# VectorE's small instructions with one SBUF tensor and pointer scalars, the head norm's constant folded into its factor, its row product and one-column moves on GpSimd

## The chip, the cores and the metric

The kernel runs on one core of a Trainium2 chip. The time is the device time of one execution in microseconds (us); lower is better. The engines are named as the profile names them: PE is TensorE (PEld its weight loads), DVE is VectorE, ACT is ScalarE, POOL is GpSimd, SP is SyncE, whose queue issues all DMAs here.

## The reference, cut to what matters

Two post-norm layers work on 1024 positions of 1024 features. A layer projects h to q, k, v and u. Eight heads of differential attention use q, k, v; each head has two softmax maps p0 and p1 over 1024 keys. u goes through a two-dimensional Fourier transform and a small linear map. Both halves are multiplied with w_o, and two layer norms stand around a SwiGLU feed-forward. The change concerns these lines of the attention:

```
p = softmax(q k^T * scale - slope * dist)          # for c = 0, 1
a = p[0] - lam * p[1]
o = a v                                            # 64 columns per head
o = o * rsqrt(mean(o^2, over the 64 columns) + 1e-5)
o = o * subln_g * (1 - lam_init)
```

and the mean, variance and shift of each layer norm. All of it is float32.

## The kernel before, in words

Positions are cut in 8 tiles of 128 partitions. Each float32 factor of a matmul is split into a high and a low part in the type fp32r that the matmuls read (`split`, L126 and L129: ScalarE writes the high part, VectorE or GpSimd subtracts), and three matmuls (`mm3`, L132 to L134) make one product.

`attention` runs over 64 blocks, 8 heads of 8 query tiles. For a block and both maps, TensorE makes the scores (L306), VectorE adds the distance and takes the row minimum (`bias_min`, L314), ScalarE takes the exponential with its row sum in a column of z (`expo`, L324). `combine` then brings both maps together without dividing: L329 takes the reciprocal of the second sum, L330 makes the column rho = z0 * (-lambda) / z1, L333 the column z0 squared on GpSimd, and E0 + rho * E1 is made in one of two ways. By the table `OFF`, 94 of the 128 blocks of both layers use two GpSimd instructions (L335, L336), the other 34 one VectorE instruction (L338). The sum is transposed on TensorE (L344), split (L351 on ScalarE, L356 on VectorE) and multiplied with v (L366).

Since nothing was divided by z0, the head norm takes it in: `norm_a` squares the head's output `onat` on GpSimd (L395), sums its 64 columns (L397), divides by 64 (L398), adds 1e-5 z0^2 (L399), takes the power -1/2 on GpSimd (L401) and multiplies the rows of `onat` with it (L402). It is called once for each of the first six heads of a layer (8 columns of factors, 512 of values) and twice for each of the last two (4 and 256). The column `subg`, the product of subln_g and 1 - lam_init, comes in later, when the heads are transposed (L416, L431).

Between the blocks stand pieces of other work from a generator, `step`, four at each block: projections of the next heads, and in the last quarter of a layer the `fourier` part. It sums and mirrors u on GpSimd (L549, L552), transposes and splits, and for each of four groups makes a pair of tiles fh and fl by a first transform, takes out of both the column at 384 (L606 copies it twice side by side into `mid`, L607 writes zero in its place), and multiplies them on TensorE in a second step. The first product reads their first half, the second their second half with the zero.

`layer_norm` (L170 to L185) makes mean and variance on VectorE (L173, L175), adds 1e-5 (L177), takes the power on GpSimd (L178) and makes the shift -mean * factor (L179); ScalarE, VectorE and GpSimd then apply it (L181 to L183).

The order on each engine is not written by hand: a scheduler places the instructions by its own model of times, within the limits that `step` gives. So a change of a few instructions may move others. Each engine runs its instructions in order.

Of the kernel before, what the change touches and what calls it, by code (L numbers as in the profile page):

```python
# [16 lines left out]
ALU = mybir.AluOpType  # L17
# [47 lines left out]
def encoder(ctx: ExitStack, tc: tile.TileContext, x, ln_in_g, ln_in_b, w_in, lam_params, subln_g,  # L65
# [35 lines left out]
    def load(o, i):  # L101
        nc.sync.dma_start(out=o, in_=i)

# [1 line left out]
    ident = sb.tile([P, P], F32, tag="ident", name="ident")  # L105
    make_identity(nc, ident)
    zero = sb.tile([P, 2], F32, tag="zero", name="zero")
# [28 lines left out]
    def load_params():  # L136
        lamp = blk("raw", (P, DEPTH, 4 * HD))
        lamm = blk("raw", (P, DEPTH, 2, HD))
        for l in range(DEPTH):
            load(bfT[:, l, :], b_f[l].rearrange("(g p) -> p g", p=P))  # L140
            for half in range(2):
                load(subg[half * VD:(half + 1) * VD, l:l + 1], subln_g[l].rearrange("(d o) -> d o", o=1))
            load(lamp[:, l, :], lam_params[l].rearrange("a d -> (a d)").partition_broadcast(P))
        lv = lamp.rearrange("p l (a b d) -> p l a b d", a=2, b=2)
        for l in range(DEPTH):
            nc.vector.tensor_tensor(out=lamm[:, l], in0=lv[:, l, :, 0, :], in1=lv[:, l, :, 1, :], op=ALU.mult)
            nc.vector.tensor_reduce(out=lams[:, l, :], in_=lamm[:, l], op=ALU.add, axis=AX.X)
            nc.scalar.activation(lams[:, l, :], lams[:, l, :], AF.Exp)
            nc.vector.tensor_tensor(out=nlam[:, l:l + 1], in0=lams[:, l, 1:2], in1=lams[:, l, 0:1], op=ALU.subtract)
            nc.vector.tensor_scalar_add(nlam[:, l:l + 1], nlam[:, l:l + 1], -LAM_INIT[l])  # L150
            nc.vector.tensor_scalar_mul(subg[:, l:l + 1], subg[:, l:l + 1], 1.0 - LAM_INIT[l])

    def load_dist(act=False):
        dist = blk("dist", (P, 2048), F16)
# [15 lines left out]
    def layer_norm(r, gb, eng=None, store=None):  # L170
        st = small([P, 2, 6], "bst", 4)
        for k in range(2):
            nc.vector.bn_stats(out=st[:, k, :], in_=r[:, k * 512:(k + 1) * 512])  # L173
        mv = small([P, 4], "bmv", 4)
        nc.vector.bn_aggr(out=mv[:, 0:2], in_=st)  # L175
        rs, nmr = mv[:, 2:3], mv[:, 3:4]
        nc.vector.tensor_scalar_add(rs, mv[:, 1:2], EPS)  # L177
        nc.gpsimd.tensor_tensor(out=rs, in0=rs, in1=mhalf, op=ALU.pow)  # L178
        nc.vector.scalar_tensor_tensor(out=nmr, in0=mv[:, 0:1], scalar=-1.0, in1=rs, op0=ALU.mult, op1=ALU.mult)  # L179
        for c in [slice(0, D)] if store is None else [slice(0, D // 2), slice(D // 2, D)]:  # L180
            nc.scalar.activation(r[:, c], r[:, c], AF.Identity, bias=nmr, scale=rs)  # L181
            nc.vector.tensor_tensor(out=r[:, c], in0=r[:, c], in1=gb[0][:, c], op=ALU.mult)
            (eng or nc.gpsimd).tensor_tensor(out=r[:, c], in0=r[:, c], in1=gb[1][:, c], op=ALU.add)  # L183
            if store is not None:
                load(store[:, c], r[:, c])  # L185
# [140 lines left out]
    def combine(blk_):  # L326
        z, es, n = blk_["z"], blk_["e"], blk_["n"]
        rho = small([P, 1], "rho", 6)
        nc.vector.reciprocal(rho, z[:, 1:2])  # L329
        nc.vector.scalar_tensor_tensor(out=rho, in0=z[:, 0:1], scalar=nlam[:, blk_["l"]:blk_["l"] + 1], in1=rho,  # L330
                                       op0=ALU.mult, op1=ALU.mult)
        z2 = blk_["head"]["z2"][:, blk_["qt"]:blk_["qt"] + 1]
        nc.gpsimd.tensor_tensor(out=z2, in0=z[:, 0:1], in1=z[:, 0:1], op=ALU.mult)  # L333
        if n % OFF[n // 16][0] < OFF[n // 16][1]:
# [57 lines left out]
    def norm_a(hd, q0, n):  # L392
        onat = hd["onat"][:, q0:q0 + n, :]
        sq = blk("on", (P, n, VD))
        nc.gpsimd.tensor_tensor(out=sq, in0=onat, in1=onat, op=ALU.mult)  # L395
        rs = small([P, n], "rs", 2)
        nc.vector.tensor_reduce(out=rs, in_=sq, op=ALU.add, axis=AX.X)  # L397
        nc.vector.tensor_scalar_mul(rs, rs, 1.0 / VD)  # L398
        nc.vector.scalar_tensor_tensor(out=rs, in0=hd["z2"][:, q0:q0 + n], scalar=EPS, in1=rs, op0=ALU.mult,  # L399
                                       op1=ALU.add)  # L400
        nc.gpsimd.tensor_tensor(out=rs, in0=rs, in1=mhalf.broadcast_to([P, n]), op=ALU.pow)  # L401
        nc.vector.tensor_tensor(out=onat, in0=onat, in1=rs.unsqueeze(2).broadcast_to([P, n, VD]), op=ALU.mult)  # L402

    def emit_half(l, h, hd, half):
        rows = slice((h % 2) * VD, (h % 2) * VD + VD)
# [122 lines left out]
    def fourier(l):  # L528
# [26 lines left out]
        for g in range(NG):  # L555
# [47 lines left out]
                  fl[:, :, 256:512].rearrange("p a (b c) -> p a b c", b=2), o, nc.scalar, nc.vector)  # L603
            mid = small([P, 2, 2], "mid", 4, F32R)
            for part, t in enumerate((fh, fl)):
                nc.vector.tensor_copy(out=mid[:, part, :], in_=f32(t[:, 1, 384:385]).broadcast_to([P, 2]))  # L606
                nc.vector.tensor_copy(out=t[:, 1, 384:385], in_=zero[:, 0:1])  # L607
            A = [t[:, 2, g * P:(g + 1) * P] for t in (hTh, hTl)]
            nB = [t[:, 2, 512 + g * P:512 + (g + 1) * P] for t in (hTh, hTl)]
            Bp = [t[:, 3, g * P:(g + 1) * P] for t in (hTh, hTl)]  # L610
# [114 lines left out]
            4: [("g0", 1), ("u0", 1)], 5: [("g0", -1), ("g1", 1)], 6: [("u1", 1)], 7: [("g0", 1)]}  # L725

    class Up:
        """gate | up projection of all positions as a 2 x 2 block product in seven block products:
        block rows are gate and up columns, the contraction and the positions are cut in halves."""

        def __init__(self, l, hs):
            self.l, self.hs = l, hs
# [116 lines left out]
    CHAIN = [("2", "11"), ("1", "11"), ("6", "12"), ("7", "22"), ("4", "21"), ("5", "22"), ("3", "12")]  # L849

    def down7(l, hs, up, pairs):
        """down projection of pairs of feature tiles, each a 2 x 2 block product in seven block products
        (block rows are the halves of the positions, block columns those of the output)."""
        B = up.B

        def fetch(n, name):
# [254 lines left out]
```

## Time and profile before

| | |
|---|---|
| median of 3 runs | 2510.63 us (2510.26 to 2516.24) |
| span of the profiled execution | 2509.6 us |
| PE busy | 2383.1 us, 95% |
| DVE busy | 1943.9 us, 77% |
| POOL busy | 1807.4 us, 72% |
| ACT busy | 1227.2 us, 49% |
| chain that ended last | PE 76%, DVE 11%, ACT 5%, POOL 3% |

The span reaches from the first to the last instruction of the program. The page gives no other time for the profiled execution, so the span stands for it; it lies 1.0 us under the median. A layer's attention runs from about 85 to 530 us and from 1323 to 1760 us, its output projection and first norm follow for some 90 us, and the feed-forward takes the rest. Busy shares are means over these stages, so they are read by stretch below. Some one-column instructions last microseconds in this profile: time that an engine spends inside an instruction counts as busy, whatever it waits for there, and shows as a long duration and not as idle time.

### The profile page before, as it was taken

Reading aid. Unit: us, or ns where it says so; the run is one execution under the profiler, and the core shown is the slowest. Engines: PE = TensorE matmul, PEld = TensorE weight load, DVE = VectorE, ACT = ScalarE, POOL = GpSimd, SP = SyncE. Lnnn points to the kernel's source line nnn. Section 1 sums busy time; section 2 is a strip of 40 time slices with the busy share of each in tenths; the row PEclk is TensorE's granted clock in tenths of the full one; section 3 lists DMA queues with packets and bytes.
Section 4 is the critical chain, followed back from the end, with each engine's and each line's share of the span. In section 5 each row is a group of like instructions: output and inputs, shape, how many; then the busy total and the mean of one; then the engine's idle time right before and its main releaser. Section 6 shows DMA issues by size and latency. Waiting matters only on the chain.

```text
span 2509.6 us, 33322 instructions
## 1 busy us (share of the span) xinstructions
PE 2383.1 (95%) x11636; PEld 1951.8 (78%) x11636; DVE 1943.9 (77%) x3003; ACT 1227.2 (49%) x2252; POOL 1807.4 (72%) x1459
## 2 busy tenths in 40 slices
PE   6999998799999999999999999888999999999997
PEld 5888776677888888888788877667778888888886
DVE  7688888756578887888768898886566887878878
ACT  4577676633344343343437766666253343333442
POOL 5476667655798888888535766676578888888873
PEclk8999999899999999999999999999999999999999
DMA  6431340231112111111324232305021111211112
GB/s 219 93 97 47 89 114 27 84 122 30 51 51 61 54 55 55 51 55 56 98 85 103 72 83 73 103 26 174 25 63 39 55 56 58 59 51 55 51 34 97
DMA packets 185783, 180.04 MB, mean 72 GB/s; under 512 B 25872, under 2 KB 149264, under 8 KB 185616
## 3 DMA queue, kind: packets, MB, share of 16 engines
q1 hardware_dynamic: 185616, 177.92, 24.7%
q8 instruction: 92, 1.51, 0.3%
q14 instruction: 75, 0.61, 0.1%
HBM read 124.39 MB, written 19.92 MB: 58 GB/s over the span
## 4 chain that ended last, share of the span: by engine, by line
PE 76%; DVE 11%; ACT 5%; issue 3%; POOL 3%; DMA 2%; SPq 0%; DVEq 0%; POOLq 0%; ACTq 0%
PE mm L134 9%; PE mm L132 9%; PE mm L133 9%; PE S L132 7%; PE S L133 7%; PE S L134 7%; PE tr L134 6%; PE tr L132 6%; PE tr L133 6%; PE mm L366 3%; DVE E L314 3%; PE S L306 3%; PE tr L344 2%; ACT E L324 2%; DVE aT L356 1%
## 5 line engine op out<-in xcount | busy, mean ns | idle before, releaser
L931 DVE TENSOR_TENSOR v<-S,v 128x512 f32<-128x512 f32 x504 | 333.6, 684 | 59.6 <-PE S L134 59.2
L324 ACT ACTIVATE E<-E,mn 128x1024 f32<-128x1024 f32 x256 | 295.5, 1155 | 103.6 <-DVE mn L314 101.8
L314 DVE CUSTOM_DVE_ANT_0 E<-S,dist 128x1024 f32<-128x1024 f32 x256 | 309.4, 1216 | 31.7 <-PE tr L344 12.1
L336 POOL TENSOR_TENSOR E<-E,E 128x1024 f32<-128x1024 f32 x94 | 225.6, 2400 | 2.8
L129 POOL TENSOR_TENSOR stk<-raw,stk 128x512 fp32r<-128x512 f32 x138 | 197.8, 1434 | 23.7 <-ACT stk L126 23.5
L132 PE MATMUL S<-w,st 128*128 128x512 f32 x544 | 212.8, 391 | 0.2
L133 PE MATMUL S<-w,st 128*128 128x512 f32 x544 | 212.9, 391 | 0.0
L134 PE MATMUL S<-w,st 128*128 128x512 f32 x544 | 212.1, 391 | 0.0
L818 DVE TENSOR_TENSOR su<-su,tr 128x512 f32<-128x512 f32 x176 | 116.4, 681 | 120.0 <-PE tr L134 116.5
L132 PE MATMUL mm<-hTh,w 128*128 128x512 f32 (+1 forms) x480 | 194.6, 405 | 13.6 <-DVE w L129 5.9
L129 POOL TENSOR_TENSOR st<-stq,st 128x512 fp32r<-128x512 f32 x126 | 194.7, 1546 | 14.7 <-ACT st L126 11.8
L356 DVE TENSOR_TENSOR aT<-tr,aT 128x512 fp32r<-128x512 f32 x256 | 172.5, 683 | 37.6 <-ACT aT L351 36.9
L134 PE MATMUL mm<-hTh,w 128*128 128x512 f32 (+1 forms) x480 | 185.0, 385 | 0.8 <-POOL w L129 0.6
L306 PE MATMUL S<-stq,stk 128*128 128x512 f32 x512 | 170.0, 422 | 15.4 <-DVE mn L314 15.1
L133 PE MATMUL mm<-hTl,w 128*128 128x512 f32 (+1 forms) x480 | 183.4, 382 | 0.2 <-DVE hTl L129 0.2
L351 ACT CAST aT<-tr 128x512 fp32r<-128x512 f32 x256 | 147.0, 585 | 66.7 <-PE tr L344 47.7
L129 POOL TENSOR_TENSOR stk<-dist,stk 128x512 fp32r<-128x512 f32 x88 | 116.2, 1320 | 77.5 <-ACT stk L126 77.4
L126 ACT CAST stk<-raw 128x512 fp32r<-128x512 f32 x138 | 85.4, 619 | 176.1 <-PE tr L134 116.8
L344 PE MATMUL tr<-ident,E 128*128 128x128 f32 x1024 | 158.1, 280 | 9.3 <-DVE aT L356 5.7
L335 POOL TENSOR_SCALAR E<-E,rho 128x1024 f32<-128x1024 f32 x94 | 105.7, 1124 | 82.3 <-DVE rho L330 47.6
L129 POOL TENSOR_TENSOR stk<-on,stk 128x512 fp32r<-128x512 f32 x88 | 123.2, 1400 | 53.8 <-ACT stk L126 53.8
L126 ACT CAST stk<-dist 128x512 fp32r<-128x512 f32 x90 | 56.0, 622 | 209.1 <-PE tr L134 126.4
(343 smaller groups left out, 7146.2 us busy)
## 6 DMA issues: line engine op xcount, KB each, us to landing
on<-in_w_gu SPq DMA_DIRECT2D x88, 256.0 KB, 2.9
raw<-in_w_gu SPq DMA_DIRECT2D x88, 256.0 KB, 2.9
raw<-in_w_in SPq DMA_DIRECT2D x64, 256.0 KB, 3.3
stq<-in_w_down SPq DMA_DIRECT2D x36, 256.0 KB, 2.8
stk<-st SPq DMA_DIRECT2D x64, 128.0 KB, 2.3
stk<-su SPq DMA_DIRECT2D x64, 128.0 KB, 2.4
stq<-st SPq DMA_DIRECT2D x64, 128.0 KB, 2.4
stq<-su SPq DMA_DIRECT2D x64, 128.0 KB, 2.5
```

The lines of the kernel that those rows point to most:

```text
L129: lo_eng.tensor_tensor(out=lo, in0=src, in1=f32(hi), op=ALU.subtract)
L132: nc.tensor.matmul(o, ah, bh, start=start, stop=False, skip_group_check=more)
L133: nc.tensor.matmul(o, ah, bl, start=False, stop=False, skip_group_check=more)
L134: return nc.tensor.matmul(o, al, bh, start=False, stop=stop, skip_group_check=more)
L306: anchor[0] = nc.tensor.matmul(s[:, half * 512:half * 512 + 512], qs[:, qt * P:qt * P + P], ks[:, half * 512:half * 512 + 512], start=True ...
L314: nc.vector.tensor_tensor_reduce(out=e, in0=s, in1=blk_["dist"][:, 896 - P * qt:896 - P * qt + S], op0=ALU.add, op1=ALU.min, scale=2.0 ** ...
L324: nc.scalar.activation(e, e, AF.Exp, bias=blk_["mn"][c], scale=-1.0, accum_out=blk_["z"][:, c:c + 1])
L336: nc.gpsimd.tensor_tensor(out=es[0], in0=es[0], in1=es[1], op=ALU.add)
L344: anchor[0] = nc.tensor.transpose(pt[:, j, :], blk_["e"][0][:, c0:c0 + P], ident)
L351: nc.scalar.copy(grp["aT"][kh][0][:, :, qq * P:qq * P + P], blk_["pt"][kh])
L356: nc.vector.tensor_tensor(out=lo[:, :, qs], in0=blk_["pt"][kh], in1=f32(hi[:, :, qs]), op=ALU.subtract)
L931: nc.vector.tensor_tensor(out=dst, in0=o, in1=dst, op=ALU.add)
```

## The change

L330 and L179 had two SBUF tensors and a scalar (`scalar_tensor_tensor`). Both become `tensor_scalar`: one tensor and two scalars, which are columns in SBUF read through a pointer (in L179 one of them a constant). L398 goes: with 64 times the sum of squares in its place, the constant in L399 is multiplied by 64, and the missing factor sqrt(64) = 8 is taken into `subg` at the start. L402, L606 and L607 are given to GpSimd. Comments and two docstrings go too. From L399 on, the lines of the changed kernel are one lower: its L398 to L401 are L399 to L402 of before, its L605 and L606 are L606 and L607, its L548 is L549.

```diff
-            nc.vector.tensor_scalar_mul(subg[:, l:l + 1], subg[:, l:l + 1], 1.0 - LAM_INIT[l])
+            nc.vector.tensor_scalar_mul(subg[:, l:l + 1], subg[:, l:l + 1], math.sqrt(VD) * (1.0 - LAM_INIT[l]))
...
-        nc.vector.scalar_tensor_tensor(out=nmr, in0=mv[:, 0:1], scalar=-1.0, in1=rs, op0=ALU.mult, op1=ALU.mult)
+        nc.vector.tensor_scalar(out=nmr, in0=mv[:, 0:1], scalar1=rs, scalar2=-1.0, op0=ALU.mult, op1=ALU.mult)
...
-        nc.vector.scalar_tensor_tensor(out=rho, in0=z[:, 0:1], scalar=nlam[:, blk_["l"]:blk_["l"] + 1], in1=rho,
-                                       op0=ALU.mult, op1=ALU.mult)
+        nc.vector.tensor_scalar(out=rho, in0=rho, scalar1=z[:, 0:1], scalar2=nlam[:, blk_["l"]:blk_["l"] + 1],
+                                op0=ALU.mult, op1=ALU.mult)
...
-        nc.vector.tensor_scalar_mul(rs, rs, 1.0 / VD)
-        nc.vector.scalar_tensor_tensor(out=rs, in0=hd["z2"][:, q0:q0 + n], scalar=EPS, in1=rs, op0=ALU.mult,
+        nc.vector.scalar_tensor_tensor(out=rs, in0=hd["z2"][:, q0:q0 + n], scalar=EPS * VD, in1=rs, op0=ALU.mult,
                                        op1=ALU.add)
         nc.gpsimd.tensor_tensor(out=rs, in0=rs, in1=mhalf.broadcast_to([P, n]), op=ALU.pow)
-        nc.vector.tensor_tensor(out=onat, in0=onat, in1=rs.unsqueeze(2).broadcast_to([P, n, VD]), op=ALU.mult)
+        nc.gpsimd.tensor_tensor(out=onat, in0=onat, in1=rs.unsqueeze(2).broadcast_to([P, n, VD]), op=ALU.mult)
...
-                nc.vector.tensor_copy(out=mid[:, part, :], in_=f32(t[:, 1, 384:385]).broadcast_to([P, 2]))
-                nc.vector.tensor_copy(out=t[:, 1, 384:385], in_=zero[:, 0:1])
+                nc.gpsimd.tensor_copy(out=mid[:, part, :], in_=f32(t[:, 1, 384:385]).broadcast_to([P, 2]))
+                nc.gpsimd.tensor_copy(out=t[:, 1, 384:385], in_=zero[:, 0:1])
```

The feed-forward keeps its order on every engine. In the attention stages the scheduler places things anew. Two places:

VectorE in the first layer, at the third Fourier group (434 to 446 us of the profile). The number behind a name tells one tile of that name from another; a tile of before has in the changed kernel a number some 6 lower, so E_4801 is E_4795 there. Before:

```order
L314 ISA mn_4832 128x1
L402 TENSOR_TENSOR on_3986<-on_3986,rs_4509 128x512
L329 RECIPROCAL rho_4937<-z_4825 128x1
L330 SCALAR_TENSOR_TENSOR rho_4937<-z_4825,nlam,rho_4937 128x1
L338 SCALAR_TENSOR_TENSOR E_4801<-E_4833,rho_4937,E_4801 128x1024
L129 TENSOR_TENSOR st_4576<-mm_4602,su_4575 128x2x256
L606 CAST mid_4663<-su_4575 128x2
```

The same blocks in the changed kernel:

```order
L329 RECIPROCAL rho_4930<-z_4819 128x1
L330 TENSOR_SCALAR rho_4930<-rho_4930,z_4819,nlam 128x1
L129 TENSOR_TENSOR w_4527<-mm_4547,w_4526 128x512
L338 SCALAR_TENSOR_TENSOR E_4795<-E_4827,rho_4930,E_4795 128x1024
L129 TENSOR_TENSOR st_4570<-mm_4571,su_4569 128x2x256
L390 TENSOR_TENSOR on_4688<-mm_4578,on_4688 128x128
```

L402 and L606 have left VectorE; L338 has moved ahead of the first L129 that writes st_4570, which stood ahead of L402 before.

GpSimd a little later, at the fourth group (464 to 472 us of the profile before). Before, L606 and L607 of this group stand on VectorE, and GpSimd has:

```order
L333 TENSOR_TENSOR z_1015_4701<-z_5100 128x1
L401 TENSOR_TENSOR rs_4873<-rs_4873,mhalf 128x4
L335 TENSOR_SCALAR E_5108<-E_5108,rho_5171 128x1024
L333 TENSOR_TENSOR z_1015_4701<-z_5148 128x1
L336 TENSOR_TENSOR E_5093<-E_5093,E_5108 128x1024
L129 TENSOR_TENSOR hTl<-raw_4905,hTh 128x256
```

In the changed kernel:

```order
L400 TENSOR_TENSOR rs_4867<-rs_4867,mhalf 128x4
L401 TENSOR_TENSOR on_4688<-on_4688,rs_4867 128x256
L605 CAST mid_4874<-st_4776 128x2
L335 TENSOR_SCALAR E_5101<-E_5101,rho_5164 128x1024
L336 TENSOR_TENSOR E_5086<-E_5086,E_5101 128x1024
L606 CAST st_4776<-zero 128x1
L605 CAST mid_4874<-su_4777 128x2
L333 TENSOR_TENSOR z_1015_4695<-z_5141 128x1
L606 CAST su_4777<-zero 128x1
L129 TENSOR_TENSOR hTl<-raw_4898,hTh 128x256
```

The row product and the four one-column instructions have come in; both zeros stand behind L335 and L336, and the second also behind L333, which waits for an exponential of ScalarE.

## Rows read from the trace of the kernel before

**Rows 1.** Windows: busy us (and instructions) of each engine, granted clock, DMA.
```profile
core 0: us, PE busy (x) PEld busy (x) DVE busy (x) ACT busy (x) POOL busy (x), PEclk, DMA share, GB/s
85.00:260.00 175.00, 172.26 (x977) 144.12 (x976) 153.15 (x294) 128.98 (x252) 117.67 (x101) 1.00 0.33 78
260.00:380.00 120.00, 111.61 (x620) 89.89 (x619) 103.41 (x186) 83.43 (x156) 77.80 (x65) 1.00 0.38 100
380.00:530.00 150.00, 122.33 (x677) 99.15 (x678) 113.78 (x202) 89.45 (x186) 96.78 (x125) 0.90 0.30 95
...
620.00:1230.00 610.00, 608.94 (x2655) 495.40 (x2654) 469.47 (x597) 245.93 (x430) 510.91 (x366) 1.00 0.19 55
...
1620.00:1760.00 140.00, 118.41 (x672) 94.44 (x672) 106.30 (x197) 89.74 (x185) 95.83 (x124) 0.93 0.31 100
```
**Rows 2.** Single lines: count, min/median/max ns, first and last start, shapes.
```profile
L330 DVE SCALAR_TENSOR_TENSOR rho<-z,nlam,rho x128: 201/220/5349, 93.2 to 1725.8; 128x1 f32<-128x1 f32 x128
...
L329 DVE RECIPROCAL rho<-z x128: 146/158/166, 92.0 to 1724.6; 128x1 f32<-128x1 f32 x128
...
L618 DVE SCALAR_TENSOR_TENSOR hTl<-mm,bfT,hTh x8: 203/205/215, 478.2 to 1716.0; 128x1 fp32r<-128x1 f32 x8
...
L177 DVE TENSOR_SCALAR bmv<-bmv x40: 93/150/156, 6.5 to 2501.2; 128x1 f32<-128x1 f32 x40
...
L179 DVE SCALAR_TENSOR_TENSOR bmv<-bmv x40: 143/159/2250, 7.4 to 2502.7; 128x1 f32<-128x1 f32 x40
```
**Rows 3.** Groups by line and shape: count | busy us, mean ns | idle us before.
```profile
L330 DVE SCALAR_TENSOR_TENSOR rho<-z,nlam,rho 128x1 f32<-128x1 f32 x128 | 63.6, 497 | 2.5
...
L338 DVE SCALAR_TENSOR_TENSOR E<-E,rho,E 128x1024 f32<-128x1024 f32 x34 | 59.2, 1741 | 0.7
...
L402 DVE TENSOR_TENSOR on<-on,rs 128x512 f32<-128x512 f32 x12 | 29.4, 2449 | 0.0
...
L398 DVE TENSOR_SCALAR rs<-rs 128x8 f32<-128x8 f32 x12 | 13.3, 1105 | 0.1
...
L395 POOL TENSOR_TENSOR on<-on 128x512 f32<-128x512 f32 x12 | 12.5, 1042 | 15.9 <-DVE on L390 14.7 <-DVE rho L329 1.1
...
L606 DVE CAST mid<-su 128x2 fp32r<-128x2 f32 x4 | 2.1, 531 | 0.0
```
**Rows 4.** Timeline of VectorE, 430 to 462: start us, us, line, operation.
```profile
434.80 3.81 DVE L402 TENSOR_TENSOR on<-on,rs 128x512 f32<-128x512 f32 x1
...
438.97 1.28 DVE L338 SCALAR_TENSOR_TENSOR E<-E,rho,E 128x1024 f32<-128x1024 f32 x1
...
445.53 0.14 DVE L607 CAST st<-zero 128x1 fp32r<-128x1 f32 x1
...
454.28 5.35 DVE L330 SCALAR_TENSOR_TENSOR rho<-z,nlam,rho 128x1 f32<-128x1 f32 x1
459.66 1.28 DVE L338 SCALAR_TENSOR_TENSOR E<-E,rho,E 128x1024 f32<-128x1024 f32 x1
```
**Rows 5.** Timeline of GpSimd in the same stretch.
```profile
434.98 2.39 POOL L336 TENSOR_TENSOR E<-E,E 128x1024 f32<-128x1024 f32 x1
...
453.23 0.22 POOL L333 TENSOR_TENSOR z<-z 128x1 f32<-128x1 f32 x1
453.38 3.37 POOL L129 TENSOR_TENSOR hTl<-raw,hTh 128x256 fp32r<-128x256 f32 x6
...
457.25 2.36 POOL L336 TENSOR_TENSOR E<-E,E 128x1024 f32<-128x1024 f32 x1
```
**Rows 6.** Timeline of TensorE: in brackets its idle us before, and what ended it.
```profile
447.50 0.48 PE L133 MATMUL mm<-st,hTh 128*128 128x512 f32 x1
...
461.60 3.78 PE L366 MATMUL mm<-aT,v 128*128 128x256 f32 x16 [6.63 <-DVE w L129]
```
**Rows 7.** The chain that ended last: start us, us, engine and line.
```profile
600.74 1.25 DVE bmv L179
...
2493.19 2.17 DVE bmv L179
```

## The prediction

> **What bounds the kernel now.** I read the busy time by stretch first [rows 1]. In the feed-forward stretch from 620 to 1230 us (its twin runs from 1850 to 2460) TensorE is busy 608.9 of 610 us at the full granted clock, and the change touches nothing there. What can be won lies in the two attention stages, 85 to 530 and 1323 to 1760. In the first of them TensorE stands idle 175 - 172.3 = 2.7 us, then 120 - 111.6 = 8.4 us, then 150 - 122.3 = 27.7 us [rows 1]: it gets worse as the projections that fill its time run out and the Fourier part, which VectorE and GpSimd prepare, takes their place. [...]
>
> The second view is the spread of single lines [rows 2]. L330 writes one column; half of its 128 runs take 0.22 us or less, the longest 5.35. L329, the reciprocal just ahead of it, reads one SBUF tensor and never takes over 0.166. L330 reads two SBUF tensors, z and rho. The third view, the timelines, shows what it waits for: it starts at 454.28 while GpSimd runs six L129 in a row, after which come a short L395 (left out there) and L336 without a pause [rows 5]; it ends at 459.63, when L336 (457.25 + 2.36) ends [rows 4]. Behind it stand L338 and the L129 that TensorE needs, and TensorE is idle 6.63 us before 461.60 [rows 6]. So a VectorE instruction with two SBUF tensors waits until GpSimd has run dry, and everything behind it on VectorE waits too.
>
> **The change, part by part.** *L330* keeps its count and gets a form with one tensor, rho, and two pointer scalars. The waits in it are 128 x (0.497 - 0.220) = 35 us [rows 2, 3]. The trace has no one-tensor instruction with two pointers. The nearest: L618 reads one SBUF tensor and one pointer beside PSUM, and its eight runs take 203 to 215 ns; L177 is the same instruction kind with constants, 93 to 156 ns, never longer [rows 2]. So the new one should cost 0.15 to 0.22, I take 0.2; the upper bound is that it still waits, and nothing is gained. Of the 35 us a part is only handed on: in 34 of the 128 blocks L338 (two SBUF tensors of 1024 columns, unchanged) comes behind L330 [rows 3]. At 454.28 it stands directly behind [rows 4], and without L330's wait it would itself wait until GpSimd's L336 ends at 459.61: 5.1 of the 35 us stay. Following the long ones through in the same way I leave 15 us handed on and 20 us gone.
>
> *L179* gets the same form. Its median is 0.159, its longest run 2.25 [rows 2]; seven of 40 wait. Four of these lie on the chain of waits that ended last: 1.25 us at 600.74, two like it (in the second layer's norm after attention, and in the first norm of all), and 2.17 at 2493.19 [rows 7]. The one at 2493 stands in the tail, where the next instructions need no second SBUF tensor, so its 2.0 us are won; the other three give 1.1 each if VectorE's next work is ready. Between 0 and 5.3 us; I take 4.
>
> *L398 goes, and L399 takes the constant.* L398's twelve runs on 8 columns took 1.105 us on average [rows 3], nearly all waiting. L399 behind it has two SBUF tensors (z2 and rs) and inherits that wait, so 20 x 0.165 = 3 us of plain work are saved, no more.
>
> *L402 moves to GpSimd.* VectorE loses 12 x 2.449 = 29.4 us [rows 3] and about 4 us for the eight of half size, 33 us, of which some two thirds is waiting: at 434.80 it took 3.81 [rows 4] while GpSimd ran L336 from 434.98 [rows 5]. Here too L338 follows (438.97), and would wait for the same L336 and what is behind it; I count 8 us as handed on, 25 gone. GpSimd gains the instruction. Its price there isn't shown; the square of the same tile, L395, takes 1.04, and half of L336 is 1.2 [rows 3, 5]. I take 1.2, so 12 x 1.2 + 8 x 0.6 = 19 us over both layers. In 380 to 530 GpSimd is busy 96.8 of 150 us [rows 1], so most of this is covered; what is queued behind it are L335 and L336, whose result TensorE transposes. I charge 2 us in all. Nobody waits for L402's own result except the store and, for the last two heads, the transposes after the attention.
>
> *L606 and L607 move to GpSimd.* The first cost up to 0.53 us on average in their group of four [rows 3]; with the zeros (0.14, [rows 4]) 9 us leave VectorE. On GpSimd a one-column move costs about 0.2, like L333 there [rows 5]: 32 x 0.2 = 6 us. The wait that this adds is the third rival below.
>
> So VectorE gets rid of 20 + 25 + 3 + 7 = 55 us in two attention stages. How much reaches the end goes by TensorE's idle time in each stretch. 85 to 260: at most 2.7 us, and mostly behind other lines; 0.7 per layer. 260 to 380: 1.3 per layer, since what L398 waited L399 will wait. The last stretches: VectorE is busy 113.8 of 150 us, and TensorE's idle spells there end with VectorE's copies. About 10 us of VectorE time per layer really go there; half of it, 5 us per layer, should reach TensorE, the rest meets the next wait. **Sum:** -4 (L179) - 1.4 - 2.6 - 10 + 2 (GpSimd) = -16 us. The sum is a difference to the profiled execution, whose span is 2509.6; the median of the runs is 2510.6, 1.0 above. **Forecast: 2495 us.** The scheduler also stirs the order in the attention stages; I give that no sign, and it is in the range.
>
> [...] In the trace L398, a one-tensor instruction with a constant, waits as the two-tensor ones do when it has 8 columns (1.105 us), while L177 with one column never does [rows 2, 3]. [...]
>
> **The rivals.** *First, the wait is handed on almost whole.* L338, L399 and L182 keep two SBUF tensors, and GpSimd has 25 us more work to wait for. For it: at both long waits in [rows 4] an L338 stands within three instructions. Against it: 94 of 128 blocks have no L338. Then 4 us of L179 and some 2 us remain: 2505. *Second, the new form still waits*, as L398 does with one tensor: L402 and the moves are about half of the 55 us, so half of the attention's 14 us is left, less the 2 on GpSimd: 5 us, 2506. L177 and L618 speak against it.
>
> *Third, slower: the zero columns come late from GpSimd.* At 445.53 VectorE writes the zero, and TensorE reads that tile at 447.50 [rows 4, 6]: 1.8 us of cover. In the new order the zeros of a layer's fourth group stand on GpSimd behind L335 and L336, of which L336 alone is 2.4 us [rows 5], and one of them behind L333, which waits for an exponential. It decides where more than 1.8 us stand ahead. If it happens in all eight groups at 2.4 us each, 19 us, and the clock drops with TensorE's idle time as it did in 380 to 530, 5 us more, against 8 us that still go: about 2526. In most groups the copies are the first that GpSimd takes after its sums, so I give it little.
>
> [...]
>
> **How the numbers follow.** Forecast (2486 to 2503) 0.43; more comes back (below 2486) 0.20; handed on 0.20; the form still waits 0.04; slower 0.13. A measurement of this kernel tells about 0.3%, 7.5 us, from no change. Faster by more than that is the first two, 0.63; within it handed on and the form, 0.24; slower 0.13. The range reaches from 2474, where half of the idle time of the last stretches and most of the clock's loss were won, to 2514, which takes in both cases of no change; I leave 0.08 below and 0.12 above. The largest unknown is how much L338 inherits, between 15 us and 35 us of L330's waits.
>
> **What would show it.** L330's longest run at 0.25 us or less, and L179's: the form is free. L338's mean above its 1.74 us of now [rows 3] by what L330 lost: handed on. The last attention stretches shorter by about 5 us each, and 85 to 260 hardly at all: the sum is right by stretch. GpSimd's zero copies as what ended TensorE's idle time: the third rival. The forecast is wrong if L330 still has runs above 1 us, or if L338 and L399 together gain more than 30 us.

## The result, and the profile after

| | before | changed |
|---|---|---|
| median of the runs, one chip | 2510.45 us | 2485.53 us (2483.11 to 2488.56) |
| ratio, 95% interval | | 0.9895 [0.9875, 0.9916] |
| span of the profiled execution | 2509.6 us | 2486.8 us |
| mean granted clock over the span | 0.982 | 0.988 |
| VectorE / GpSimd / TensorE busy, us | 1943.9 / 1807.4 / 2383.1 | 1862.5 / 1839.9 / 2366.5 |

The kernel is faster by 1.05%, 25 us between the medians. A second comparison (experiment 5) gave 0.9874 [0.9858, 0.9891], 31 us, and a profile with a span of 2478.6 us at a clock of 0.990. The two intervals overlap; both profiles are used below, and the one of experiment 5 is called the second profile.

The first view is the one by stretches, of the changed kernel; the columns are those of [rows 1].

```profile
85.00:260.00 175.00, 168.89 (x938) 140.19 (x937) 141.95 (x285) 126.52 (x246) 117.85 (x99) 0.99 0.31 74
260.00:380.00 120.00, 112.75 (x635) 93.78 (x636) 91.58 (x183) 83.34 (x159) 88.13 (x76) 0.97 0.41 106
380.00:530.00 150.00, 128.30 (x742) 103.15 (x741) 106.90 (x193) 95.22 (x193) 106.22 (x144) 0.98 0.30 97
620.00:1230.00 610.00, 607.25 (x2637) 493.81 (x2636) 472.45 (x593) 245.40 (x427) 510.79 (x366) 1.00 0.19 57
1620.00:1760.00 140.00, 117.69 (x662) 95.42 (x662) 92.04 (x164) 81.78 (x164) 101.56 (x128) 0.96 0.32 100
```

Beside [rows 1]: in 380 to 530 us TensorE's idle time went from 27.7 to 21.7 us and the granted clock from 0.90 to 0.98. In 1620 to 1760 us the idle time stayed (21.6 and 22.3 us), and the clock went from 0.93 to 0.96. It isn't all gain: in 85 to 260 TensorE is idle 6.1 us instead of 2.7, and in 260 to 380 the clock fell from 1.00 to 0.97.

Fixed stretches of the two profiles don't hold the same work (380 to 530 has 677 matmuls of TensorE before and 742 after). So here are the same pieces of work in each kernel, cut at the first score matmul (L306) of a block, up to the last L366 of a layer, in us:

| stage | before | L330 alone (experiment 1) | changed, first and second profile |
|---|---|---|---|
| start, to the first block | 86.5 | 86.6 | 84.0, 82.6 |
| layer 1, blocks 1 to 24 | 126.6 | 127.0 | 132.8, 130.5 |
| layer 1, blocks 25 to 48 | 147.2 | 143.4 | 143.3, 142.8 |
| layer 1, blocks 49 to 64 | 158.5 | 157.3 | 145.3, 143.2 |
| from there to layer 2's first block | 805.3 | 801.7 | 803.3, 802.9 |
| layer 2, blocks 1 to 24 | 127.3 | 126.9 | 127.4, 127.1 |
| layer 2, blocks 25 to 48 | 147.2 | 144.4 | 144.0, 145.4 |
| layer 2, blocks 49 to 64 | 150.9 | 148.1 | 146.4, 144.8 |
| from there to the end | 760.1 | 761.5 | 760.3, 759.3 |

Most of the gain lies in the last 16 blocks of layer 1. What the clock takes can be bounded from the span and its mean: the share below 1.00, times the span. Before that is 2509.6 x 0.018 = 45 us, in the changed kernel 2486.8 x 0.012 = 30 us, in its second profile 2478.6 x 0.010 = 25 us. These are upper bounds, since they count time at the lower level (0.50; the traces of the kernel before and of the changed one have this level and 1.00 alone) in which TensorE is idle or, behind its last matmul, done (5.7, 4.4 and 5.0 us of them). In the trace before, 128x512 matmuls back to back start 0.43 us apart at 0.50 (441.93 to 443.21) and 0.23 apart at 1.00 (700.12 to 702.91), so about half of the busy time at the lower level is lost: 31.5, 21.8 and 18.6 us. So the clock gave back 10 to 15 of the 22.8 us between the first two spans, and 13 to 20 of the 31.0 to the second profile. TensorE's own times agree: with the same 11636 matmuls it is busy for 16.6 and 18.1 us less, and idle for 6.2 and 12.9 us less.

The second view is that of the single lines, of the changed kernel (min/median/max in ns; L398, L401, L605, L606 here are L399, L402, L606, L607 of before).

```profile
L330 DVE TENSOR_SCALAR rho<-rho,z,nlam x128: 259/272/276, 92.2 to 1699.1; 128x1 f32<-128x1 f32 x128
...
L179 DVE TENSOR_SCALAR bmv<-bmv x40: 198/213/217, 7.4 to 2479.9; 128x1 f32<-128x1 f32 x40
```

Neither form ever waits: the longest run of L330 is 0.276 us where it was 5.349, that of L179 0.217 where it was 2.25 [rows 2]. Each has one pointer more and one tensor less than the old form, and its median run is 0.05 us longer than that of the old one. The third view gives the groups (count | busy us, mean ns | idle us before), of the changed kernel.

```profile
L338 DVE SCALAR_TENSOR_TENSOR E<-E,rho,E 128x1024 f32<-128x1024 f32 x34 | 55.3, 1626 | 0.3
L330 DVE TENSOR_SCALAR rho<-rho,z,nlam 128x1 f32<-128x1 f32 x128 | 34.6, 271 | 2.9
L398 DVE SCALAR_TENSOR_TENSOR rs<-z,rs 128x8 f32<-128x8 f32 x12 | 10.3, 855 | 0.1
...
L401 POOL TENSOR_TENSOR on<-on,rs 128x512 f32<-128x512 f32 x12 | 12.6, 1049 | 0.3
L401 POOL TENSOR_TENSOR on<-on,rs 128x256 f32<-128x256 f32 x8 | 4.9, 611 | 0.2
L606 POOL CAST su<-zero 128x1 fp32r<-128x1 f32 x8 | 3.7, 457 | 0.0
```

L338 did not take over what L330 lost: 55.3 us in 34 runs, 59.2 before [rows 3]. The row product costs GpSimd 12.6 + 4.9 = 17.5 us and takes 33 us from VectorE. In 380 to 530 us TensorE's longest idle spell is now the second of these, where 6.63 us stood before [rows 6]. The first one is longer and just ahead of that stretch: TensorE waits 3.7 us for the transfer of in_w_f (2.8 us in the second profile, 1.6 before), so a part of the gain is lost there (timelines of TensorE, changed kernel):

```profile
373.59 2.05 PE L541 MATMUL mm<-raw,raw 128*128 128x512 f32 x2 [3.71 <-DMA raw<-in_w_f]
...
431.54 0.33 PE L132 MATMUL mm<-hTh,w 128*128 128x128 f32 x1 [1.94 <-DVE st L129]
```

### The profile page after: what moved, and what is told of

The parts are those of the page before. It is cut to its first block, busy times and chain, and to the rows that moved or that the text cites. A ratio compares the mean times of both kernels' runs of the same rounds, so it can differ in the third digit from the quotient of the medians.

```text
span 2486.8 us, 33290 instructions
## 1 busy us (share of the span) xinstructions
PE 2366.5 (95%) x11636; PEld 1944.9 (78%) x11636; DVE 1862.5 (75%) x2931; ACT 1228.7 (49%) x2252; POOL 1839.9 (74%) x1511
## 4 chain that ended last, share of the span: by engine, by line
PE 78%; DVE 8%; POOL 4%; DMA 3%; issue 3%; ACT 2%; SPq 2%; DVEq 0%; POOLq 0%; ACTq 0%
PE mm L132 10%; PE mm L134 9%; PE mm L133 9%; PE S L132 7%; PE S L133 7%; PE S L134 7%; PE tr L134 6%; PE tr L132 6%; PE tr L133 6%; PE S L306 3%; PE mm L366 3%; PE tr L344 3%; DVE E L314 2%; SPq L102 2%; DVE v L182 1%
## 5 line engine op out<-in xcount | busy, mean ns | idle before, releaser
L314 DVE CUSTOM_DVE_ANT_0 E<-S,dist 128x1024 f32<-128x1024 f32 x256 | 310.3, 1218 | 56.2 <-PE tr L344 22.4
L336 POOL TENSOR_TENSOR E<-E,E 128x1024 f32<-128x1024 f32 x94 | 227.3, 2419 | 3.5
L129 POOL TENSOR_TENSOR stk<-raw,stk 128x512 fp32r<-128x512 f32 x138 | 197.0, 1428 | 22.2 <-ACT stk L126 22.0
L356 DVE TENSOR_TENSOR aT<-tr,aT 128x512 fp32r<-128x512 f32 x256 | 174.0, 685 | 44.5 <-ACT aT L351 44.2
L129 POOL TENSOR_TENSOR st<-stq,st 128x512 fp32r<-128x512 f32 x126 | 194.8, 1547 | 14.5 <-ACT st L126 11.8
L306 PE MATMUL S<-stq,stk 128*128 128x512 f32 x512 | 167.9, 419 | 17.6 <-DVE mn L314 16.1
L129 POOL TENSOR_TENSOR stk<-dist,stk 128x512 fp32r<-128x512 f32 x88 | 116.3, 1321 | 76.3 <-ACT stk L126 75.0
L129 POOL TENSOR_TENSOR stk<-on,stk 128x512 fp32r<-128x512 f32 x88 | 123.6, 1404 | 53.1 <-ACT stk L126 53.1
L335 POOL TENSOR_SCALAR E<-E,rho 128x1024 f32<-128x1024 f32 x94 | 106.2, 1130 | 75.3 <-DVE rho L330 46.8
```

The lines of the kernel that those rows point to most:

```text
L129: lo_eng.tensor_tensor(out=lo, in0=src, in1=f32(hi), op=ALU.subtract)
L306: anchor[0] = nc.tensor.matmul(s[:, half * 512:half * 512 + 512], qs[:, qt * P:qt * P + P], ks[:, half * 512:half * 512 + 512], start=True ...
L314: nc.vector.tensor_tensor_reduce(out=e, in0=s, in1=blk_["dist"][:, 896 - P * qt:896 - P * qt + S], op0=ALU.add, op1=ALU.min, scale=2.0 ** ...
L336: nc.gpsimd.tensor_tensor(out=es[0], in0=es[0], in1=es[1], op=ALU.add)
L356: nc.vector.tensor_tensor(out=lo[:, :, qs], in0=blk_["pt"][kh], in1=f32(hi[:, :, qs]), op=ALU.subtract)
```

## The experiments

Two theories stood at the start. **Waits:** VectorE no longer waits in small instructions until GpSimd has run dry, so what TensorE needs comes earlier. **Order:** the scheduler's new order of the attention stages did it. Beside them stood the forecast's own idea that the waits are partly **handed on**. All ratios are against the kernel before on the same chip; experiments 1 to 8 ran on one chip, 9 to 12 on another.

**1. L330's form alone.** The kernel before with

```
-  nc.vector.scalar_tensor_tensor(out=rho, in0=z[:, 0:1], scalar=nlam[...], in1=rho, ...)
+  nc.vector.tensor_scalar(out=rho, in0=rho, scalar1=z[:, 0:1], scalar2=nlam[...], ...)
```

> The kernel before with L330's new form alone (one SBUF tensor, two pointer scalars). Theory A, the waits go and the gain is theirs: L330's longest run is under 0.3 us, L338's mean stays at about 1.7 us, the granted clock of the last attention stretches rises, and the time falls by 12 to 17 us, more than half of the 25 us of the whole change. Theory B, the forecast's step: L338 takes over some 15 us of the waits (its mean over 34 runs rises from 1.74 to about 2.2 us), and the time falls by about 8 us. Theory C, the new order of the instructions did it: L330 is free as in A, but the time goes up or down by up to 5 us, with no relation to the waits.

0.9941 [0.9922, 0.9960], 15 us. L330 is free (longest 0.276 us), and the groups show that nothing behind it took the wait:

```profile
L338 DVE SCALAR_TENSOR_TENSOR E<-E,rho,E 128x1024 f32<-128x1024 f32 x34 | 60.3, 1773 | 0.5
...
L402 DVE TENSOR_TENSOR on<-on,rs 128x512 f32<-128x512 f32 x12 | 28.4, 2365 | 0.0
```

1.1 us more in L338, 1.0 less in L402: not the 15 of the forecast. This one line brings about half of the change's gain. The clock is 0.984, which bounds what it takes at 40 us: at most 5 of the 12.9 us by which the span is shorter. Theory A's sign, a higher clock in the last stretches, hardly came (0.90 to 0.91 in 380 to 530, 0.93 to 0.95 in 1620 to 1760). By the stages above, the gain lies in blocks 25 to 48 and behind the attention, and the last 16 blocks of layer 1 win 1.2 us.

**2. The row product alone.** The kernel before with

```
-  nc.vector.tensor_tensor(out=onat, in0=onat, in1=rs.unsqueeze(2)..., op=ALU.mult)
+  nc.gpsimd.tensor_tensor(out=onat, in0=onat, in1=rs.unsqueeze(2)..., op=ALU.mult)
```

> The kernel before with only the row product (L402) on GpSimd. VectorE loses 33 us of busy time, GpSimd gets 17 to 18. Theory A: what waited at L402 mostly goes, L330 goes on waiting (mean about 0.5 us or more), and the time falls by 5 to 8 us. Theory B, handed on: L330, L338 and L399 behind it take over the wait (together some 10 us more), the time falls by 0 to 3 us. Theory C, order: up or down by up to 5 us.

0.9989 [0.9975, 1.0003]: nothing that can be told from no change, for 33 us less on VectorE. L330 takes 6 us more than before (63.6 us there):

```profile
L330 DVE SCALAR_TENSOR_TENSOR rho<-z,nlam,rho 128x1 f32<-128x1 f32 x128 | 69.9, 546 | 2.9
```

**3. All of the change but L330.** The changed kernel with the first line of experiment 1 put back.

> The changed kernel with L330 in its old form (two SBUF tensors). Theory A: L330 waits again, with a mean of 0.5 us or more, since GpSimd has more to do; the time is 12 to 17 us above the changed kernel, about 2500. If the parts help each other or stand for the same waits, the sum of this run's gain and that of L330 alone differs from 25 us. Theory C, order: the time lies within 5 us of the changed kernel's.

0.9998 [0.9986, 1.0011]. Without L330 the whole rest is worth nothing, and by the ratios the time is 26 to 31 us above the changed kernel, beyond the 12 to 17 expected. L330 took over 13 us:

```profile
L330 DVE SCALAR_TENSOR_TENSOR rho<-z,nlam,rho 128x1 f32<-128x1 f32 x128 | 76.9, 601 | 2.8
```

So there is handing on, but to L330 and not from it. In the blocks of L335 its result is what GpSimd waits for: GpSimd stands idle for 41.0 us, in 34 places, until L330 has written rho. How much of that reaches TensorE was not measured.

**4. Another order alone, before.** The kernel before with

```
-  rho = small([P, 1], "rho", 6)
-  nc.vector.reciprocal(rho, z[:, 1:2])
+  rh2 = small([P, 2], "rho", 6)
+  nc.vector.reciprocal(rh2, z)
+  rho = rh2[:, 1:2]
```

> The kernel before with nothing of the change; the reciprocal L329 takes both columns of z in place of one, which costs a few nanoseconds and makes the scheduler place about a hundred of TensorE's instructions in the attention stages elsewhere. Theories A and B: the time stays within 2 us of before, since the waits of L330 and L402 are there as before. Theory C: a new order alone moves the time by 5 us or more, to either side.

0.9991 [0.9977, 1.0005]. The order is new, and the time does not move. But this order differs less from before than that of experiment 1: in the traces 264 of TensorE's 11636 places hold another matmul (by operation and tile names), in experiment 1 it is 1181. What speaks against the order more strongly are all runs together: in the four kernels with the old L330 (before, 2, 3, 4) the ratio is 0.9989 or more, in the nine with the new one 0.9964 or less, whatever order the scheduler made. The counterpart on the changed kernel is experiment 11.

**5. The whole change again**, beside the next three.

> The changed kernel itself, on the chip of the runs beside it. All theories: 0.990 of before, 0.988 to 0.992, some 25 us.

0.9874 [0.9858, 0.9891], as said above.

**6. L330 and the row product, nothing else.** Both edits of experiments 1 and 2.

> The kernel before with L330's new form and the row product on GpSimd, nothing else. L330 alone brought 15 us, the row product alone at most 3, the change without L330 nothing. Theory A2, the two waits stand in for each other (without L402, L330 waited 6 to 13 us more): with both gone the row product's 33 us count as well, and this kernel has 20 us or more of the 25. Theory D, the rest of the gain comes from the small parts (shift of the norm, folded constant, one-column moves): this kernel gains no more than L330 alone, about 15 us, 0.994.

0.9932 [0.9916, 0.9947], 17 us: no more than L330 alone within the intervals. Here another instruction took the wait, L606, the copy of two columns (group, then timelines of VectorE, GpSimd and TensorE, in brackets idle us before):

```profile
L606 DVE CAST mid<-su 128x2 fp32r<-128x2 f32 x8 | 13.0, 1625 | 0.0
```
```profile
428.65 0.69 DVE L129 TENSOR_TENSOR st<-mm,su 128x512 fp32r<-128x512 f32 x1
429.26 3.67 DVE L606 CAST mid<-su 128x2 fp32r<-128x2 f32 x1
432.85 1.27 DVE L338 SCALAR_TENSOR_TENSOR E<-E,rho,E 128x1024 f32<-128x1024 f32 x1
434.04 0.68 DVE L356 TENSOR_TENSOR aT<-tr,aT 128x512 fp32r<-128x512 f32 x1
...
427.35 2.56 POOL L549 TENSOR_TENSOR st<-su 128x512 f32<-128x512 f32 x2
429.84 2.38 POOL L336 TENSOR_TENSOR E<-E,E 128x1024 f32<-128x1024 f32 x1
432.16 0.75 POOL L549 TENSOR_TENSOR su<-st 128x256 f32<-128x256 f32 x1
...
434.77 1.11 PE L344 MATMUL tr<-ident,E 128*128 128x128 f32 x4 [3.73 <-DVE aT L356]
```

The copy starts at 429.26 and ends at 432.93, when GpSimd's last instruction of the row ends (432.16 + 0.75). L338 and L356 stand behind it, and TensorE is idle for 3.73 us. With L330 free and the row product gone, L606 is where VectorE waits next in this order. Experiment 8 asks whether that alone counts.

**7. All of the change but the row product.** The row product back on VectorE.

> The changed kernel with the row product (L401 here, L402 of before) back on VectorE. Theory A2: it waits there again (mean about 2.4 us), nothing else takes the wait over, and 5 to 10 us of the gain are lost: 0.993 to 0.994. Theory D: the time is within 3 us of the changed kernel, 0.990.

0.9887 [0.9868, 0.9906], its interval overlapping that of the whole. Where it stands now the product waits less than before (groups; before, 29.4 and 4.1 us):

```profile
L401 DVE TENSOR_TENSOR on<-on,rs 128x512 f32<-128x512 f32 x12 | 18.5, 1538 | 0.3 <-POOL rs L400 0.3
...
L401 DVE TENSOR_TENSOR on<-on,rs 128x256 f32<-128x256 f32 x8 | 5.9, 741 | 7.9 <-POOL rs L400 7.9
```

With experiment 2: the largest of the edits by VectorE's time, 33 us, brings nothing that these runs can show, alone or last.

**8. All but the one-column moves.** L605 and L606 of the changed kernel back on VectorE.

> The changed kernel with the one-column moves (L605, L606 here) back on VectorE. The third rival in small: in the changed kernel TensorE waits about 1 us per layer for the zero column from GpSimd, so the time should fall by 1 to 3 us. Against it: VectorE has 32 more instructions, of which some wait (6.4 + 2.3 us before), and the time rises by 1 to 4 us. Its order is nearly that of the changed kernel, so theory C gives less than 3 us either way.

0.9896 [0.9877, 0.9914]: as the whole in its first comparison, 5 us above its second, the intervals overlapping. Its copies wait 5 us in all, those of experiment 6 15 us. So neither is it borne out that the zeros on GpSimd cost something that putting them back would save, nor that the moves alone bring something that these runs can show.

**9. All but the shift of the layer norm.** L179 in its old form.

> The changed kernel with L179, the shift of the layer norm, in its old form (two SBUF tensors). The profiles so far: outside the two attention stages the kernels with the new L179 need 3.6 to 8.7 us less than before, those with the old one 0.3 to 2.2 us less. Theory A, the waits on the chain of the norms are L179's: its longest run is again above 1 us, the stretches outside attention grow by 4 us or so, and the time is 3 to 6 us above the changed kernel. Theory B, the next instruction with two SBUF tensors (L182) takes the wait over: the time stays within 2 us of the changed kernel.

0.9892 [0.9871, 0.9913], between nothing and 4.5 us above the whole's two ratios, overlapping. The profiles show where L179 counts and where not. At the start: the first L306 runs at 84.0 and 82.6 us in the whole's two profiles and at 87.0 here (86.5 before); over all profiles it is 84.8 to 87.0 with the old form and 82.4 to 84.3 with the new one. At the end: from the last norm's first L179 to the end of the program it takes 38.2 us in the whole, 40.0 here and before. In the norm after attention the wait is handed on to L182, which adds two SBUF tensors. The chain of this kernel, and then of the whole's second profile (start us, us):

```profile
585.04 1.25 DVE bmv L179
...
587.59 1.24 DVE v L182
```
```profile
581.09 0.22 DVE bmv L179
...
582.62 2.03 DVE v L182
```

1.25 + 1.24 against 0.22 + 2.03: of the 1.03 us won, 0.79 went to L182.

**10. All but the folded constant.** The changed kernel with

```
+  nc.vector.tensor_scalar_mul(rs, rs, 1.0 / VD)
-  ... scalar=EPS * VD ...
+  ... scalar=EPS ...
```

and the factor of `subg` without its 8.

> The changed kernel with the division by 64 (L398 of before) back on VectorE. Theory D2, what the two large parts lack beside the shift (5 of 15 us) comes from the fold and the moves, since one instruction that waits less lets the chain of the head norm end earlier: the time is 3 to 8 us above the changed kernel. Theory B, the forecast's: the wait is L399's anyway, only 3 us of plain work come back on an engine that is not the bound: within 3 us of the changed kernel. Theory C, the new order (some 400 of TensorE's instructions stand elsewhere): up to 8 us either way, with no more waiting in L398 and L399 together than the changed kernel has in its L398 (13 us).

0.9964 [0.9949, 0.9979]: 17 to 23 us above the whole's two ratios, and 15 to 18 us above experiments 9, 11 and 12 beside it; no theory had that much. L398 and L399 together take 8 us more than L398 of the changed kernel, but the larger item is L338 (group, then the timelines of VectorE, GpSimd and TensorE around its longest run):

```profile
L338 DVE SCALAR_TENSOR_TENSOR E<-E,rho,E 128x1024 f32<-128x1024 f32 x34 | 65.4, 1923 | 0.7
```
```profile
433.32 0.27 DVE L330 TENSOR_SCALAR rho<-rho,z,nlam 128x1 f32<-128x1 f32 x1
433.63 5.61 DVE L338 SCALAR_TENSOR_TENSOR E<-E,rho,E 128x1024 f32<-128x1024 f32 x1
439.15 0.68 DVE L129 TENSOR_TENSOR st<-mm,su 128x512 fp32r<-128x512 f32 x1
...
432.30 1.05 POOL L402 TENSOR_TENSOR on<-on,rs 128x512 f32<-128x512 f32 x1
433.30 2.40 POOL L336 TENSOR_TENSOR E<-E,E 128x1024 f32<-128x1024 f32 x1
435.65 2.50 POOL L549 TENSOR_TENSOR st<-su 128x512 f32<-128x512 f32 x2
438.09 1.19 POOL L606 CAST mid<-su 128x2 fp32r<-128x2 f32 x1
...
439.89 0.80 PE L132 MATMUL mm<-su,hTh 128*128 128x512 f32 x1 [3.81 <-DVE st L129]
```

L330 is free and L338 stands right behind it and waits through L336 and two L549: the forecast's handing on, in the order of this kernel. The copy behind it on VectorE (L129) is what TensorE waits 3.81 us for. The clock is 0.982, as before the change, which again bounds its part at 45 us. What is not settled: this kernel differs from the changed one by the 20 short instructions and by some 400 of TensorE's instructions that stand elsewhere. Whether the fold matters through its own waits (8 us) or because the scheduler happened to put L338 behind GpSimd's long row was not separated; a kernel with the old instruction in the changed kernel's order was not run.

**11. Another order alone, changed kernel.** The edit of experiment 4 on the changed kernel.

> The changed kernel with the reciprocal L329 on both columns of z, which costs a few nanoseconds and makes the scheduler place some 200 of TensorE's instructions in the attention stages elsewhere. Theory A: within 3 us of the changed kernel. Theory C: an order alone is worth 5 us or more, to either side; then differences of that size between the other kernels can't be given to their edit.

0.9903 [0.9884, 0.9923], 2 to 7 us above the whole's two ratios, the intervals overlapping. So an order alone may be worth up to some 0.3% here, and differences of that size (experiments 7, 8 and 9) are not given to their edits. Those of experiments 1, 3 and 10 against their partners are two to four times as large.

**12. One step more.** The changed kernel with

```
-  nc.gpsimd.tensor_tensor(out=z2, in0=z[:, 0:1], in1=z[:, 0:1], op=ALU.mult)
+  nc.gpsimd.tensor_scalar(out=z2, in0=z[:, 0:1], scalar1=z[:, 0:1], scalar2=EPS * VD, ...)
...
-  nc.vector.scalar_tensor_tensor(out=rs, in0=hd["z2"]..., scalar=EPS * VD, in1=rs, ...)
+  nc.gpsimd.tensor_tensor(out=rs, in0=rs, in1=hd["z2"]..., op=ALU.add)
```

> The changed kernel and one step more of the same kind: z0 squared is multiplied with its constant where it is made (L332, on GpSimd, with pointer and constant in place of two tensors), and the sum with the squares (L398) is a plain addition on GpSimd in place of a VectorE instruction with two SBUF tensors. Theory A: VectorE loses the 13 us that L398 takes in the changed kernel (10.3 us in 12 runs on 8 columns, 2.9 in 8 on 4), GpSimd gets 20 additions of about 0.2 us, and the time falls by 1 to 5 us. Theory B: the wait there was covered, the time stays within 2 us. Theory C, order: up to 8 us either way.

0.9906 [0.9887, 0.9925]: the 13 us left VectorE and the time did not fall. No version here is faster than the changed kernel by more than the intervals.

**All runs side by side.** The waiting is worked out from the traces: in L330, L338, L398, L399, L402, L606, L179 and L149 (a two-tensor instruction at the start), what each run on VectorE took beyond the short runs of its form, summed (lines as numbered before). "Lost" is the span times the share of the clock below 1.00, the upper bound from above. Both are of one profile; the clock of the kernel before lies between 0.981 and 0.987 over its runs, so 8 us of "lost" are no difference.

| kernel | ratio | waiting, us | of it L330 / L338 | clock | lost, us |
|---|---|---|---|---|---|
| before | 1 | 108 | 36 / 16 | 0.982 | 45 |
| 4 order only | 0.9991 | 116 | 41 / 16 | 0.983 | 43 |
| 2 row only | 0.9989 | 91 | 42 / 18 | 0.983 | 43 |
| 3 all but L330 | 0.9998 | 78 | 49 / 17 | 0.982 | 45 |
| 1 L330 only | 0.9941 | 72 | 1 / 17 | 0.984 | 40 |
| 6 L330 and row | 0.9932 | 53 | 0 / 13 | 0.987 | 32 |
| 7 all but row | 0.9887 | 39 | 0 / 14 | 0.990 | 25 |
| 10 all but fold | 0.9964 | 38 | 0 / 22 | 0.982 | 45 |
| 9 all but shift | 0.9892 | 33 | 1 / 11 | 0.987 | 32 |
| 8 all but moves | 0.9896 | 32 | 1 / 11 | 0.984 | 40 |
| 11 whole, order | 0.9903 | 26 | 1 / 12 | 0.984 | 40 |
| changed, twice | 0.9895, 0.9874 | 23, 23 | 0 / 12 | 0.988, 0.990 | 30, 25 |
| 12 one step more | 0.9906 | 13 | 1 / 12 | 0.988 | 30 |

The time follows the sum of the waiting only loosely: 30 us less of it in experiment 3 brought nothing, and 10 us less in experiment 12 neither. The two kernels that stand off the trend have the most waiting in L330 (3) and in L338 (10), the two instructions that lead to the tile that TensorE transposes, and behind which the copies that TensorE reads are queued. That these two weigh more than the others is read from the table and not shown: no run changed one of them alone at the same order, and experiment 6 doesn't follow it, with 13 us in the two as in the kernels near 0.990 and a ratio of 0.9932. There L606 holds 15 us.

## Why the prediction was right, and where its steps were not

The forecast was 2495 us, 16 us less than before; the direction and the range held, and the gain was 25 us, in the second comparison 31. The measured 2485.5 lies just outside the band that the forecast gave itself (2486 to 2503), in that of "more comes back". What carried it is that the new forms don't wait (longest runs 0.276 and 0.217 us). That the sum came as near as it did is partly luck, since its terms missed to both sides. VectorE's busy time fell by 81 us where 55, and 4 of L179, were counted. L330's 20 of the 55 stood for about 5 of the attention's 14 us and bring 15 alone; the row product's 25 bring nothing that the runs can show. Step by step:

- **L330's form: right.** It never waits. It costs 0.27 and not 0.2 us (the sign asked for 0.25), 9 us more on VectorE in all.
- **15 of 35 us handed on to L338: wrong for this change.** L338 lost 4 us, and in experiment 1 gained 1.1. The step followed one place, 454.28, "in the same way" to all others. Counted in the trace before, 28 runs of L330 above 0.6 us hold 30.6 us of waiting, and L338 is the next instruction behind 6 of them, with 7.9 us. Behind the others come L356, L129, L390, L314 or L618, which take one operand from PSUM and did not wait (0.68, 0.28, 0.28, 1.21 to 1.23 and 0.21 us there); where L338 came one later, as behind the waits at 249 and 1347 us, it ran in its plain 1.27 us. Experiment 10 shows that the step names something real: there L338 waits 22 us.
- **L179, -4 us: about right in size, from other places.** By the profiles, some 3 us at the start (by the first L306, the wait of L149 among them) and 1.8 us in the tail are won. The norms after attention give little, since L182 takes the wait. The time of experiment 9 can't show a gain of this size.
- **The fold, 3 us: the term that is open.** The two instructions took 23.3 us before, the one left takes 13.1: 10 us, not 3, so the wait was not inherited whole. Experiment 10 puts 15 to 23 us on it, together with its order.
- **The row product: price right, worth wrong.** 17.5 us on GpSimd (19 forecast) and 33 off VectorE as said. The forecast took 25 of the 33 as gone and let them carry the largest part of the relief. Experiments 2 and 7 find no gain. Only the store and the last heads wait for its result, as the text itself had said, and 6 us of its waits came up again in L330 while that still could wait.
- **The moves: small, with something behind.** They take 8.2 us on GpSimd (6 forecast). The forecast saw 9 us on VectorE; in experiment 6, with the other waits gone, the same L606 waits 15 us, in experiment 8 it waits 5.
- **From VectorE to the end: the step that was mis-sized.** -10 us were to come as less idle time of TensorE in the last stretches, 5 in each layer. The last 16 blocks are 13.2 and 15.3 us shorter in layer 1 (of which idle time 6.4 and 6.7, the clock while TensorE was busy 6.5 and 9.1), and 4.5 and 6.1 in layer 2 (idle time 1.5 more and 1.7 less, the clock 4.3 and 2.7). So layer 2 is as forecast in size, and layer 1 has the clock on top: that is "more comes back", which had 0.20. The lower end of the range, 2474, counts most of the clock's loss in the last stretches as won; no run shows that term. Over the whole span the runs bound the loss at 45 us before, of which 10 to 15 us came back. Blocks 25 to 48 win 2 to 4 us in each layer (1.3 was forecast for 260 to 380), and blocks 1 to 24 of layer 1 lose 4 to 6 us, which was not forecast. Why the clock rose is told only in part: before, TensorE was idle for 6.63 us from 455.0, and from 457.0 to 467.2 us the clock was at 0.50, its lower level; in 380 to 530 no spell above 2 us is left. In layer 2's last stretch the spells above 1 us add up to more than before (15.3 us, 10.6 before), and the clock rose all the same.

Of the other rivals: the new form does not wait, so the second fell. The third came only in small: TensorE waits about 1 us in each layer behind a zero of L606, whose longest run on GpSimd is 1.26 us, not 2.4 us in eight groups; the 5 us that it added for the clock were an estimate that no run shows, and the clock rose from 0.982 to 0.988. The first is wrong as it was put, though the waits do pass between instructions (experiments 2, 3, 6, 9 and 10).

## What to carry to other kernels

When VectorE waits for GpSimd inside short instructions, the waits of several lines can stand for each other: taking one line out brought nothing here while L330 could still wait (experiments 2 and 3, ratios 0.9989 and 0.9998), and 15 us when it was L330 itself (experiment 1). Look at each long run for the very next instruction and for who waits behind it, and do not scale one place up to all. Where the granted clock of a stretch is below 1.00, price what a change may give back in clock beside the idle time: here it was 10 to 15 of 22.8 us. Compare the same pieces of work and not the same stretch of time, and count the lower clock only where TensorE works.

## What the runs showed of the hardware

**With one SBUF tensor, one column never waited; two, four and eight did, but not in every instruction.** L607 writes one column from one SBUF tensor and took at most 0.155 us in every profile with it on VectorE. L606 beside it is the same instruction with two columns and one SBUF tensor, and took up to 3.69 us in experiment 6; L398 waits with four and eight (means of 0.43 and 1.11 us in the profile before, where its shortest run took 0.159). The reciprocal L329 did not: in experiments 4 and 11 it reads and writes two columns, and its 128 runs took at most 0.168 and 0.169 us, while L330 right behind it took up to 5.4 us in experiment 4. The single lines of L606 in experiment 6, of L607 there, and of L329 in experiment 4:

```profile
L606 DVE CAST mid<-su x8: 159/1244/3692, 393.3 to 1684.7; 128x2 fp32r<-128x2 f32 x8
...
L607 DVE CAST su<-zero x8: 140/142/153, 393.7 to 1686.0; 128x1 fp32r<-128x1 f32 x8
...
L329 DVE RECIPROCAL rho<-z x128: 147/160/168, 91.0 to 1727.8; 128x2 f32<-128x2 f32 x128
```

So the new forms are probably free because they have one column as much as because they have one tensor; a new form on two columns was not run. Why a single column does not wait was not shown.

**The wait runs through several GpSimd instructions**, not one: L606 in experiment 6 for 3.67 us, through the rest of L549, L336 and another L549. In the trace before, 43 of L330's 128 runs took more than 0.45 us, and each of them ended 2 to 20 ns after the end of a GpSimd instruction. Not every GpSimd instruction is waited for: eight runs of L330 that took 0.22 us lie inside one of L401. **And it goes the other way as well.** In experiment 5 (timeline of VectorE, then of GpSimd):

```profile
106.70 3.39 DVE L338 SCALAR_TENSOR_TENSOR E<-E,rho,E 128x1024 f32<-128x1024 f32 x1
...
106.58 2.42 POOL L336 TENSOR_TENSOR E<-E,E 128x1024 f32<-128x1024 f32 x1
108.94 1.20 POOL L333 TENSOR_TENSOR z<-z 128x1 f32<-128x1 f32 x1
```

L338, which takes 1.27 us when it does not wait, ends at 110.09, 1.09 us after the end of L336 at 109.00; L333, one column that mostly takes 0.19 us, lasts until 110.14. GpSimd's L333 went from 31.0 to 36.2 us in all with the change, so a part of what VectorE no longer waits is waited there.
